# A decoder trunk in fp32: the additions behind seven products spread over more side steps, and the input loads put at the head of the queue

## The chip, the cores and the metric

The kernel runs on one core of one Trainium2 chip. The metric is the device time of one execution in microseconds; the median of three runs stands for a kernel. A profile is one further execution, recorded by the hardware profiler.

## What is computed

A two-layer trunk over 512 positions of width 2048, in fp32. Each layer is a half feed-forward block, a pair of mixers (attention in both layers, with a pooling mixer in the second), and another half feed-forward block, each behind an RMS norm and added to the residual. A last RMS norm gives the output. The part that matters here is the feed-forward block, with an inner width of 1536:

```python
def swiglu(x, w_gate, w_up, w_down):
    return (jax.nn.silu(x @ w_gate) * (x @ w_up)) @ w_down

h = h + 0.5 * swiglu(rms_norm(h, norm_g[i, 0]), ffn_w_gate[i, 0], ffn_w_up[i, 0], ffn_w_down[i, 0])
```

There are four such blocks. The first one is computed in the plain way (`ffn`), the other three by `ffn_products`.

## The kernel before

**Precision.** TensorE multiplies fp32r here. Every fp32 operand is therefore split into a high part (ScalarE, a copy, L273 for weights) and the rest (VectorE, a subtraction, L274), and a product is three matmuls: high by high, high by rest, rest by high (`mm3`, L302 to L304).

**Weights.** All weights come in a fixed sequence of tiles of at most 128x512 (`plan_and_uses`). A tile is loaded by SyncE's DMA queue into one of 9 buffers `raw` (L258) and split into one of 7 pairs `wh`, `wl`. `take` splits a tile six places ahead of the one that it hands to TensorE (`ahead`), so the split of tile i+6 stands on ScalarE and VectorE just ahead of the work that follows tile i. The load of a tile stands on SyncE's queue behind the release of the buffer nine tiles earlier.

**Three blocks with seven products.** The inner width is done in three units of 512 columns. For a unit, `w_gate` and `w_up` over the two halves of the 2048 rows, and the input over its two halves of positions, make a 2x2 by 2x2 block product, which is done with seven products instead of eight. Some weight tiles are first added to or subtracted from each other (L278). A unit has two passes. In the first (PSUM tiles `pa`), 24 weight tiles go through three products; in the second (`pb`), 32 tiles go through four. Each tile serves six matmuls of 128x128 by 512 columns. At the end of a pass the products are copied or added to SBUF tiles `s` (L612, L618).

**The additions.** What is left of a unit is `to_hidden` (L620 on), a generator: eight additions on VectorE (L622) and four Silu on ScalarE (L626, L629), then four multiplications on VectorE (L636) that give four tiles of rows, then, for each of four groups of 128 columns, four transposes of these rows on TensorE (L644, PSUM tile `ht`) and a split of the result into `hidh`, `hidl` (L312, L313). It is put into the deque `side` when the unit ends, and runs beside the next unit: each `tick()` advances it to its next `yield`. In the first pass of the next unit there is a tick behind each of the 24 weight tiles. Behind the third unit comes the down projection instead: its first four output tiles do the two units that are ready in eight half steps of 12 matmuls (`pd`), with two ticks behind each, then the deque is emptied (`while side: tick()`), and then the rest of these four tiles is done from the third unit.

The order of instructions on each engine is the order in which this code issues them; an engine works through its own in that order and waits where an operand isn't there.

**Start.** `load_x` (L349 to L352) loads the 16 tiles of the input, 128x512 each, on SyncE's queue, among the weight tiles. The first block needs x0 to x3 for its first four weight tiles, x4 to x7 for the next four, and so on. `beside(i)`, called behind weight tile i of the first block, splits input tile i+4 (`xgh` on ScalarE L315, `xgl` on VectorE L316) and adds the square of tile i to the norm's sum (ScalarE L387, GpSimd L395).

Of the kernel before, what the change touches and what calls it, by code (L numbers as in the profile page):

```python
# [216 lines left out]
def trunk(ctx: ExitStack, tc: tile.TileContext, xT, pos_row, pos_col, wts, gains, consts, bias_a_in, bias_b_in, outT):  # L217
# [19 lines left out]
    def blk(s, dt=F32):  # L237
        return bpool.tile([P, S], dt, tag="b", name=nm(s))

    def bank(s):  # L240
        return psum.tile([P, S], F32, tag="p", name=nm(s))
# [11 lines left out]
    def load_to(i):  # L253
        while nxt_load[0] <= min(i, len(plan) - 1):
            j = nxt_load[0]
            off, n = offsets[j]
            t = raws.tile([P, 512], F32, tag="raw", name=f"raw_{j}")
            nc.sync.dma_start(t[:, :n], wts[off:off + P * n].rearrange("(p n) -> p n", p=P))  # L258
            raw_t[j] = t
            nxt_load[0] += 1  # L260
# [25 lines left out]
    def take(name, n):  # L286

        while n:
            i = nxt_use[0]
            r = plan[i]  # L290
            assert r[0] == name and r[4] - r[3] <= n, (i, r, name, n)
            ahead()
            h, low = split_t.pop(i)
            w = offsets[i][1] // (r[4] - r[3])
            for k in range(r[4] - r[3]):
                c = slice(k * w, (k + 1) * w)
                yield r[3] + k, h[:, c], low[:, c]
            n -= r[4] - r[3]
            nxt_use[0] += 1

    def mm3(out, ah, al, bh, bl, start, stop):
        nc.tensor.matmul(out, ah, bh, start=start, stop=False)  # L302
        nc.tensor.matmul(out, ah, bl, start=False, stop=False)  # L303
        nc.tensor.matmul(out, al, bh, start=False, stop=stop)  # L304
# [34 lines left out]
    def finish(g):  # L339
        for _ in g:  # L340
            pass
# [7 lines left out]
    def load_x(d0, d1):  # L349
        for d in range(d0, d1):  # L350
            xs[d] = blk(f"x{d}")
            nc.sync.dma_start(xs[d], xT[d * P:(d + 1) * P, :])  # L352

    nc.scalar.dma_start(gn, gains)
    load_x(0, 4)
    load_to(2)
    load_x(4, 8)
    nc.scalar.dma_start(cs, consts)
    ident = cs[:, 0:P]
    mask_d = cs[:, P:2 * P]  # L360
# [16 lines left out]
    class Norm:  # L377
# [7 lines left out]
        def add(self, x, last=False):  # L385
            sq = blk("sq")[:, :self.m]
            nc.scalar.activation(sq, x, AF.Square)  # L387
            acc = self.accs[self.count % self.sums] if len(self.accs) >= self.sums else None
            self.count += 1
            if last or acc is None:  # L390
                self.accs.append(sq)
            elif self.by_dma:
                nc.gpsimd.dma_start(acc, sq, accum_op=ALU.add)
            else:
                nc.gpsimd.tensor_tensor(acc, acc, sq, op=ALU.add)  # L395
# [135 lines left out]
    def down_half(pd, job, hid, n):  # L531
        _, c0, c1 = job
        for k, wh, wl in take("ffn_w_down", n):
            mm3(pd[:, :c1 - c0], wh, wl, hid[k][0][:, c0:c1], hid[k][1][:, c0:c1], k == 0, k == NF - 1)
# [60 lines left out]
    def ffn_products(pieces, norm, resid_in, sink, down):  # L595
        hid = {}
        ng = norm.stages()
        both = range(2)
        late = pieces.late()

        def product(names, piece, ps, k, u):
            for kk, wh, wl in take(names, 1):
                assert kk % HK == k
                sh, sl = pieces.get(k, piece, u == FF // UNIT - 1)
                for a in both:
                    c = slice(a * P, a * P + P)
                    mm3(ps[a], sh[:, c], sl[:, c], wh, wl, k == 0, k == HK - 1)

        def copied(ps):
            out = [blk("s") for _ in both]  # L610
            for a in both:
                nc.scalar.activation(out[a], ps[a], AF.Copy)  # L612
            return out

        def added(ps, s, into=None):
            out = [blk("s") if into is None else into[a] for a in both]
            for a in both:
                nc.vector.tensor_tensor(out[a], ps[a], s[a], op=ALU.add)  # L618
            return out

        def to_hidden(u, c11, u2, s4, s5, s7, c12):
            add = lambda o, a, b: nc.vector.tensor_tensor(o, a, b, op=ALU.add)  # L622
            for a in both:
                add(s7[a], s7[a], u2[a])
                add(s4[a], s4[a], s7[a])
                nc.scalar.activation(s4[a], s4[a], AF.Silu, scale=norm.r[:, a:a + 1])  # L626
                yield
                add(s7[a], s7[a], s5[a])
                nc.scalar.activation(s7[a], s7[a], AF.Silu, scale=norm.r[:, 2 + a:3 + a])  # L629
                add(c12[a], c12[a], s5[a])  # L630
                yield
            u2.clear()
            s5.clear()
            for a in both:
                for o, g, r in ((c11, s4, a), (c12, s7, 2 + a)):
                    nc.vector.scalar_tensor_tensor(o[a], o[a], norm.r[:, r:r + 1], g[a], op0=ALU.mult, op1=ALU.mult)  # L636
                yield
            s4.clear()
            s7.clear()
            rows = c11 + c12  # L640
            for f in range(UNIT // P):
                pt = bank("ht")
                for b in range(NST):
                    nc.tensor.transpose(pt[:, b * P:b * P + P], rows[b][:, f * P:f * P + P], ident)  # L644
                yield
                hid[u * (UNIT // P) + f] = split(pt, "hid")

        for u in range(FF // UNIT):
            p1, p2, p4 = ([bank("pa") for _ in both] for _ in range(3))
            last = HK - 1  # L650
            for k in range(HK):
                product("ffn_w_up", "B11", p1, k, u)
                if k == last:
                    s1 = copied(p1)
                if u == 0:
                    for e in range(k + 1, min(k + 4, HK)):
                        pieces.get(e, "B11", False)
                else:
                    tick()
                product("ffn_w_up", "B21", p2, k, u)  # L660
                if k == last:
                    c11 = added(p2, s1)
                if u == 0:
                    next(late, None)
                else:
                    tick()
                product("ffn_w_gate", "T4", p4, k, u)
                if k == last:
                    s4 = copied(p4)
                if u:  # L670
                    tick()
                elif k > HK // 2:
                    next(ng, None)
            if u == 0:
                finish(ng)
                finish(late)
            del p1, p2, p4
            p5, p7, p6, p3 = ([bank("pb") for _ in both] for _ in range(4))
            for k in range(HK):
                product("ffn_w_gate", "T1", p5, k, u)  # L680
                if k == last:
                    s5 = copied(p5)
                if k % 2:
                    tick()
                product("ffn_w_gate", "T3", p7, k, u)
                if k == last:
                    s7 = copied(p7)
                if k % 2:
                    tick()
                product("ffn_w_up", "T2", p6, k, u)  # L690
                if k == last:
                    u2 = added(p6, s1, s1)
                if k % 2:
                    tick()
                product("ffn_w_up", "B22", p3, k, u)
                if k % 2:
                    tick()
            side.append(to_hidden(u, c11, u2, s4, s5, s7, added(p3, u2)))
            del p5, p7, p6, p3, s1, c11, u2, s4, s5, s7
        pds = [bank("pd") for _ in range(FIRST)]  # L700
        for pd, job in zip(pds, down):
            for n in (4, 4):
                down_half(pd, job, hid, n)
                tick(2)
        while side:
            tick()
        for pd, job in zip(pds, down):
            down_half(pd, job, hid, 4)
            down_done(pd, job, resid_in, sink)
        for job in down[FIRST:]:  # L710
            pd = bank("pd")
            for n in (8, 4):
                down_half(pd, job, hid, n)
                tick()
            down_done(pd, job, resid_in, sink)
# [222 lines left out]
        xg[d] = split(xs[d], "xg", scale=g_norm(0)(d))  # L938

    def beside(i):  # L940
        if i in (0, 3):
            load_x(8 if i == 0 else 12, 12 if i == 0 else 16)
        if i + 4 < NK:
            split_x(i + 4)
        norm.add(xs[i])
# [277 lines left out]
```

## Time and profile before

| | |
|---|---|
| median of 3 runs | 2327.6 us (2327.45 to 2329.95) |
| the profiled execution, its own time | 2328.22 us |
| its span, first to last instruction | 2326.4 us |
| TensorE matmuls (PE), busy | 2249.4 us, 97% |
| VectorE (DVE), busy | 1450.0 us, 62% |
| ScalarE (ACT), busy | 1051.5 us, 45% |
| mean granted TensorE clock | 0.984 |

In a row of the waits stand: engine, what it was about to write and its line, what it waited for; microseconds in total, times, longest. In a row of a timeline: start in us, busy us, engine, line, operation, output<-inputs, shape, count of merged instructions, and in brackets the idle time just before and what ended it. `SPq` is SyncE's DMA queue. In a row of the windows: from:to and length in us, then busy us and number of instructions of each engine, the granted clock (PEclk, 1.00 is full), the DMA share and GB/s.

### The profile page before, as it was taken

The page shows a single profiled execution, that of the slowest core. Times are in us where ns is not written, and L with a number is a line of the kernel's source. Part 1 is how long each engine was busy: PE and PEld are TensorE (multiplying, and loading weights), DVE is VectorE, ACT ScalarE, POOL GpSimd, SP SyncE. Part 2 cuts the span into 40 slices and gives each one's busy share as a digit, 9 for nine tenths or more (in the row PEclk, how much of TensorE's full clock was granted, in tenths as well). Part 3 has the DMA queues.
Part 4 walks back from the last instruction along what each step waited for, and adds up shares of the span by engine and source line. Part 5 has one row for each costly group of instructions (what it writes and reads, how often), then busy time and mean ns, then how long its engine had stood idle before and what let it go on. Part 6 is the DMA issues. An engine that isn't in the chain of part 4 may idle for free.

```text
span 2326.4 us, 30133 instructions
## 1 busy us (share of the span) xinstructions
PE 2249.4 (97%) x10364; PEld 1882.2 (81%) x10364; DVE 1450.0 (62%) x2460; ACT 1051.5 (45%) x1875; POOL 185.7 (8%) x191
## 2 busy tenths in 40 slices
PE   8999999999999999889999898999999999898997
PEld 6888888989888888778788787788888888687787
DVE  5453344464645688878557787755345679788634
ACT  5332333333334575445446454433235576454443
POOL 3000011000001011000011000011200011000013
PEclk9999999999999999999999999999999999999999
DMA  6333343423224486556676565554332486565544
GB/s 219 100 87 105 104 127 114 122 64 104 74 73 124 134 250 185 166 153 185 179 192 182 165 189 152 156 181 151 98 96 69 127 238 200 154 181 164 148 140 142
DMA packets 193290, 336.94 MB, mean 145 GB/s; under 512 B 21488, under 2 KB 44400, under 8 KB 193136
## 3 DMA queue, kind: packets, MB, share of 16 engines
q1 hardware_dynamic: 163184, 280.89, 40.9%
q10 hardware_dynamic: 23904, 43.11, 5.7%
q0 software_dynamic: 6048, 11.01, 2.9%
q8 instruction: 81, 1.33, 0.2%
q14 instruction: 73, 0.60, 0.1%
HBM read 298.75 MB, written 25.17 MB: 139 GB/s over the span
## 4 chain that ended last, share of the span: by engine, by line
PE 87%; DVE 5%; issue 3%; ACT 2%; DMA 2%; POOL 0%; DVEq 0%; ACTq 0%; POOLq 0%
PE pd L303 7%; PE pd L304 7%; PE pd L302 7%; PE pb L302 5%; PE pb L304 5%; PE pb L303 5%; PE pj L302 4%; PE pj L304 4%; PE pj L303 4%; PE pa L302 3%; PE pa L303 3%; PE pa L304 3%; PE wo L302 3%; PE wo L304 3%; PE wo L303 3%
## 5 line engine op out<-in xcount | busy, mean ns | idle before, releaser
L274 DVE TENSOR_TENSOR wl<-raw,wh 128x512 fp32r<-128x512 f32 (+3 forms) x1087 | 737.2, 688 | 605.1 <-ACT wh L273 569.2
L273 ACT ACTIVATE wh<-raw 128x512 fp32r<-128x512 f32 (+3 forms) x1087 | 652.5, 609 | 749.5 <-DVE wl L274 126.3
L302 PE MATMUL pd<-hidh,wh 128*128 128x512 f32 (+1 forms) x816 | 307.9, 377 | 0.0
L304 PE MATMUL pd<-hidh,wl 128*128 128x512 f32 (+1 forms) x816 | 307.3, 377 | 0.0
L303 PE MATMUL pd<-hidl,wh 128*128 128x512 f32 (+1 forms) x816 | 307.3, 377 | 0.0
L278 DVE TENSOR_TENSOR raw<-raw,raw 128x512 f32<-128x512 f32 x288 | 196.6, 683 | 0.0
L302 PE MATMUL pj<-xgh,wh 128*128 128x512 f32 x464 | 181.7, 392 | 0.0
L304 PE MATMUL pj<-xgh,wl 128*128 128x512 f32 x464 | 180.8, 390 | 0.0
L303 PE MATMUL pj<-xgl,wh 128*128 128x512 f32 x464 | 180.7, 389 | 0.0
L302 PEld LDWEIGHTS pd<-hidh,wh 128*128 128x128 f32 x816 | 153.6, 188 | 28.1
L303 PEld LDWEIGHTS pd<-hidl,wh 128*128 128x128 f32 x816 | 153.6, 188 | 28.0
L304 PEld LDWEIGHTS pd<-hidh,wl 128*128 128x128 f32 x816 | 153.6, 188 | 27.8
L302 PE MATMUL pa<-wh,pbh 128*128 128x512 f32 x432 | 175.1, 405 | 0.0
L395 POOL TENSOR_TENSOR sq<-sq,sq 128x512 f32<-128x512 f32 (+1 forms) x65 | 81.5, 1253 | 1155.8 <-ACT sq L387 1155.8
L303 PE MATMUL pa<-wl,pbh 128*128 128x512 f32 x432 | 171.6, 397 | 0.0
L304 PE MATMUL pa<-wh,pbl 128*128 128x512 f32 x432 | 171.3, 397 | 0.0
L302 PE MATMUL pb<-wh,pth 128*128 128x512 f32 x288 | 112.2, 390 | 0.9 <-DVE s L618 0.9
L304 PE MATMUL pb<-wh,ptl 128*128 128x512 f32 x288 | 112.0, 389 | 0.0
L303 PE MATMUL pb<-wl,pth 128*128 128x512 f32 x288 | 112.0, 389 | 0.0
L304 PEld LDWEIGHTS pj<-xgh,wl 128*128 128x128 f32 x464 | 87.1, 188 | 18.2
L303 PEld LDWEIGHTS pj<-xgl,wh 128*128 128x128 f32 x464 | 87.2, 188 | 17.4
L302 PEld LDWEIGHTS pj<-xgh,wh 128*128 128x128 f32 x464 | 87.2, 188 | 17.3
(265 smaller groups left out, 3941.6 us busy)
## 6 DMA issues: line engine op xcount, KB each, us to landing
raw<-wts SPq DMA_DIRECT2D x940, 256.0 KB, 2.8
spill<-x ACTq DMA_DIRECT2D x80, 256.0 KB, 3.0
x<-spill ACTq DMA_DIRECT2D x80, 256.0 KB, 3.1
raw<-wts SPq DMA_DIRECT2D x83, 192.0 KB, 2.4
sq<-sq POOLq DMA_DIRECT2D x42, 256.0 KB, 4.9
raw<-wts SPq DMA_DIRECT2D x48, 128.0 KB, 2.4
x<-xT SPq DMA_DIRECT2D x16, 256.0 KB, 5.0
outT<-sc SPq DMA_DIRECT2D x16, 256.0 KB, 2.3
```

Source lines behind the costliest of these rows:

```text
L273: nc.scalar.activation(h, src, AF.Copy)
L274: nc.vector.tensor_tensor(low, src, f32(h), op=ALU.subtract)
L278: nc.vector.tensor_tensor(to, a, b, op=ALU.add if sign > 0 else ALU.subtract)
L302: nc.tensor.matmul(out, ah, bh, start=start, stop=False)
L303: nc.tensor.matmul(out, ah, bl, start=False, stop=False)
L304: nc.tensor.matmul(out, al, bh, start=False, stop=stop)
L395: nc.gpsimd.tensor_tensor(acc, acc, sq, op=ALU.add)
```

## The change

Two things. In `to_hidden` more `yield` statements are put in: where a step of additions or multiplications was followed by one, there are now two, and one more stands ahead of the transposes. The generator has 17 of them where it had 10. And the 16 input tiles are all loaded at the start, four at a time with two weight tiles behind each four; `beside` loads none any more.

```diff
     nc.scalar.dma_start(gn, gains)
-    load_x(0, 4)
-    load_to(2)
-    load_x(4, 8)
+    for i in range(4):
+        load_x(4 * i, 4 * i + 4)
+        load_to(2 * i + 2)
...
                 nc.scalar.activation(s4[a], s4[a], AF.Silu, scale=norm.r[:, a:a + 1])
                 yield
+                yield
                 add(s7[a], s7[a], s5[a])
                 nc.scalar.activation(s7[a], s7[a], AF.Silu, scale=norm.r[:, 2 + a:3 + a])
                 add(c12[a], c12[a], s5[a])
+                yield
                 yield
...
                     nc.vector.scalar_tensor_tensor(o[a], o[a], norm.r[:, r:r + 1], g[a], op0=ALU.mult, op1=ALU.mult)
                 yield
+                yield
             s4.clear()
             s7.clear()
+            yield
...
     def beside(i):
-        if i in (0, 3):
-            load_x(8 if i == 0 else 12, 12 if i == 0 else 16)
         if i + 4 < NK:
             split_x(i + 4)
```

**TensorE, the first pass of the second unit** (the first of six such places). Before, these rows stand behind 7 of the pass's 24 weight tiles, that is behind 42 matmuls; `wh_8382` is the seventh tile, and `s` are the four tiles of rows:

```order
L304 MATMUL pa_8377<-wh_8382,pbl_7233 128x512
L644 MATMUL ht_8482<-cs,s_7919 128x128
L644 MATMUL ht_8482<-cs,s_7920 128x128
L644 MATMUL ht_8482<-cs,s_8372 128x128
L644 MATMUL ht_8482<-cs,s_8373 128x128
L302 MATMUL pa_8378<-wh_8397,pbh_7236 128x512
```

Now they stand behind 14 tiles, that is behind 84 matmuls; `wh_8478` is the fourteenth tile:

```order
L304 MATMUL pa_8379<-wh_8478,pbl_7405 128x512
L648 MATMUL ht_8566<-cs,s_7919 128x128
L648 MATMUL ht_8566<-cs,s_7920 128x128
L648 MATMUL ht_8566<-cs,s_8372 128x128
L648 MATMUL ht_8566<-cs,s_8373 128x128
L302 MATMUL pa_8380<-wh_8490,pbh_7400 128x512
```

The same four transposes moved by seven weight tiles; the three groups behind them still follow one per tile. Beside the down projection the first group moved from behind four half steps to behind seven, and the last three groups now stand in one piece behind the eighth, just ahead of the matmuls that use them.

**VectorE, the same place.** Before, one split of a weight tile (L274) stands between two steps of the additions:

```order
L274 TENSOR_TENSOR wl_8383<-raw_8258,wh_8382 128x512
L622 TENSOR_TENSOR s_8342<-s_8342,s_7902 128x512
L622 TENSOR_TENSOR s_7943<-s_7943,s_8342 128x512
L274 TENSOR_TENSOR wl_8398<-raw_8270,wh_8397 128x512
L622 TENSOR_TENSOR s_8342<-s_8342,s_8326 128x512
L622 TENSOR_TENSOR s_8372<-s_8372,s_8326 128x512
L274 TENSOR_TENSOR wl_8413<-raw_8282,wh_8412 128x512
L622 TENSOR_TENSOR s_8343<-s_8343,s_7903 128x512
```

Now there are two:

```order
L274 TENSOR_TENSOR wl_8383<-raw_8258,wh_8382 128x512
L622 TENSOR_TENSOR s_8342<-s_8342,s_7902 128x512
L622 TENSOR_TENSOR s_7943<-s_7943,s_8342 128x512
L274 TENSOR_TENSOR wl_8398<-raw_8270,wh_8397 128x512
L274 TENSOR_TENSOR wl_8410<-raw_8282,wh_8409 128x512
L622 TENSOR_TENSOR s_8342<-s_8342,s_8326 128x512
L622 TENSOR_TENSOR s_8372<-s_8372,s_8326 128x512
L274 TENSOR_TENSOR wl_8425<-raw_8294,wh_8424 128x512
L274 TENSOR_TENSOR wl_8437<-raw_8306,wh_8436 128x512
L622 TENSOR_TENSOR s_8343<-s_8343,s_7903 128x512
```

From the first addition to the last multiplication five more splits stand in between. ScalarE's high parts follow the same pattern between its Silu. Beside the down projection, where two ticks followed each split, one step now stands between two splits.

**SyncE's queue, the start.** Before, behind the input tiles x4 to x7 (the last of them is `x_8`), these weight tiles follow, the fourth to the ninth:

```order
L352 DMA x_8_100<-xT 128x512
L258 DMA raw_112<-wts 128x512
L258 DMA raw_114<-wts 128x512
L258 DMA raw_116<-wts 128x512
L258 DMA raw_118<-wts 128x512
L258 DMA raw_120<-wts 128x512
L258 DMA raw_122<-wts 128x512
```

Now two weight tiles follow, then the input tiles x8 to x11, two weight tiles, and the next input tiles:

```order
L352 DMA x_8_100<-xT 128x512
L258 DMA raw_102<-wts 128x512
L258 DMA raw_104<-wts 128x512
L352 DMA x_9_106<-xT 128x512
L352 DMA x_10_108<-xT 128x512
L352 DMA x_11_110<-xT 128x512
L352 DMA x_12_112<-xT 128x512
L258 DMA raw_114<-wts 128x512
L258 DMA raw_116<-wts 128x512
L352 DMA x_13_118<-xT 128x512
```

Before, x8 to x11 stood behind 16 weight tiles and x12 to x15 behind 19. The sixth and seventh weight tile now have four more input tiles ahead of them, the eighth and ninth eight more.

## The prediction

> **What bounds the kernel now.** First the page, for the engine that sets the time:
>
> ```profile
> span 2326.4 us, 30133 instructions
> PE 2249.4 (97%) x10364; PEld 1882.2 (81%) x10364; DVE 1450.0 (62%) x2460; ACT 1051.5 (45%) x1875; POOL 185.7 (8%) x191
> ```
>
> TensorE works through 97% of the span, so what can be won here lies in its gaps. The waits of TensorE name them:
>
> ```profile
> PE ht L644 <- DVE s L636: 53.4, 21, 7.3
> PE gu L303 <- DVE xgl L316: 2.4, 1, 2.4
> ```
>
> The transposes wait 53.4 us for VectorE's rows, nearly all that TensorE waits for. The order shows nine such places: six passes and three starts of a down projection. The windows give the length of each from its first matmul on. First the six units with two passes, of which three and the sum are shown:
>
> ```profile
> 920.25:1009.77 89.52, 80.78 (x354) 66.05 (x352) 70.45 (x112) 44.91 (x73) 0.00 (x0) 0.94 0.60 165
> 1009.77:1098.23 88.46, 81.05 (x354) 66.27 (x352) 70.46 (x112) 43.63 (x72) 0.00 (x0) 0.94 0.59 166
> 1994.55:2084.51 89.96, 81.22 (x354) 66.38 (x352) 70.45 (x112) 45.08 (x73) 0.00 (x0) 0.94 0.57 164
> sum 532.83, PE 485.67 PEld 397.04 DVE 422.63 ACT 264.97 POOL 0.00; mean PE 80.95 PEld 66.17 DVE 70.44 ACT 44.16 POOL 0.00
> ```
>
> Then the three starts of a down projection, up to the ninth half step, one and the sum:
>
> ```profile
> 1098.23:1124.51 26.28, 24.18 (x114) 19.62 (x112) 18.02 (x29) 9.57 (x16) 0.00 (x0) 1.00 0.35 94
> sum 78.76, PE 72.48 PEld 58.81 DVE 54.05 ACT 28.72 POOL 0.00; mean PE 24.16 PEld 19.60 DVE 18.02 ACT 9.57 POOL 0.00
> ```
>
> The granted clock of 0.94 in the passes says that each also runs at half clock for a while. TensorE's timeline in the second of these units shows why:
>
> ```profile
> 1009.77 0.39 PE L302 MATMUL pa<-wh,pbh 128*128 128x512 f32 x1
> ...
> 1019.06 0.39 PE L304 MATMUL pa<-wh,pbl 128*128 128x512 f32 x1
> 1025.40 0.47 PE L644 MATMUL ht<-cs,s 128*128 128x128 f32 x1 [5.96 <-DVE s L636]
> 1027.33 1.14 PE L644 MATMUL ht<-cs,s 128*128 128x128 f32 x3 [1.45 <-DVE s L636]
> 1028.12 0.78 PE L302 MATMUL pa<-wh,pbh 128*128 128x512 f32 x1
> 1028.70 0.63 PE L303 MATMUL pa<-wl,pbh 128*128 128x512 f32 x1
> 1029.12 0.63 PE L304 MATMUL pa<-wh,pbl 128*128 128x512 f32 x1
> ...
> 1033.37 0.60 PE L644 MATMUL ht<-cs,s 128*128 128x128 f32 x4
> ...
> 1035.20 0.60 PE L644 MATMUL ht<-cs,s 128*128 128x128 f32 x4
> ```
>
> From 1009.77 to 1019.06 start 42 matmuls, 41 steps of 0.227 us, so a weight tile (six) takes 1.36. Behind seven tiles the transposes come and stand for about 8 us. Then matmuls start 0.42 to 0.43 apart, half the pace. An undisturbed group of transposes is read at the end: 1.83 us from group to group, less 1.36, is 0.47.
>
> So a unit without loss would be 56 tiles x 1.36 + 4 x 0.47 = 78.05 us, six of them 468.3; lost are 532.8 - 468.3 = 64.5 us, of it the waits and the slow clock behind them. A down start would be 8 x 12 x 0.227 + 4 x 0.47 = 23.7, three 71.0; lost are about 7.8 us. Together 72.3 us can be won, and no more.
>
> **The additions: where they end.** VectorE and ScalarE in the same pass, their timelines:
>
> ```profile
> 1012.14 0.68 DVE L274 TENSOR_TENSOR wl<-raw,wh 128x512 fp32r<-128x512 f32 x1
> 1012.74 1.41 DVE L622 TENSOR_TENSOR s<-s,s 128x512 f32<-128x512 f32 x2
> 1015.46 0.69 DVE L274 TENSOR_TENSOR wl<-raw,wh 128x512 fp32r<-128x512 f32 x1 [1.31 <-DMA raw<-wts]
> 1016.07 1.28 DVE L622 TENSOR_TENSOR s<-s,s 128x512 f32<-128x512 f32 x2
> ...
> 1026.53 1.41 DVE L636 SCALAR_TENSOR_TENSOR s<-s,r,s 128x512 f32<-128x512 f32 x2
> 1027.86 1.28 DVE L274 TENSOR_TENSOR wl<-raw,wh 128x512 fp32r<-128x512 f32 x2
> ```
>
> ```profile
> 1014.18 0.72 ACT L626 ACTIVATE s<-s,r 128x512 f32<-128x512 f32 x1 [3.58 <-DVE s L622]
> 1014.81 0.61 ACT L273 ACTIVATE wh<-raw 128x512 fp32r<-128x512 f32 x1
> ...
> 1023.35 2.17 ACT L273 ACTIVATE wh<-raw 128x512 fp32r<-128x512 f32 x4
> ```
>
> This is a chain that hands over between the two engines: additions at 1012.74, Silu at 1014.18, the next high part queued behind it at 1014.81, its rest at 1015.46 (the wait is put down to a load, but the high part had just started), the next additions at 1016.07. It doesn't wait for TensorE, and ends at 1027.94, 18.17 us after the pass began. The change puts one more split into each of the five gaps. Its high part follows the other 0.52 later ((2.17 - 0.61) / 3) and is hidden; its rest takes VectorE's pace, 0.60 (1012.14 to 1012.74). So the chain grows by 5 x 0.60 = 3.0 and ends at 21.17.
>
> TensorE now reaches the transposes behind 14 tiles, at 14 x 1.36 = 19.04. Before, it resumed 0.18 behind the chain's end (1028.12); so it resumes at 21.35 instead of 19.04 + 0.47 = 19.51, a loss of 1.84 us. Where the wait goes, the weights could be late next. The rest of tile 11 (counted from 0) starts behind the third step: that step was at 1018.67 - 1009.77 = 8.90, becomes 10.10, then two additions and Silu (1.44), 0.63 and 0.65 make 12.82, ready at 13.5; TensorE wants it at 14.96. Tile 13 is ready at 16.7, wanted at 17.68. The cover is 1 us.
>
> ```profile
> 1018.67 1.41 DVE L622 TENSOR_TENSOR s<-s,s 128x512 f32<-128x512 f32 x2
> ```
>
> Two of the six have one instruction more on ScalarE (x73):
>
> ```profile
> 924.70 1.28 ACT L626 ACT_TABLE_LOAD   x1 [3.62 <-DVE s L622]
> ```
>
> With its handover it puts the chain back by 1.33 (Silu at 926.00 - 920.25 = 5.75, against 1014.18 - 1009.77 = 4.41). There the loss is 3.17, and tile 13 comes some 0.2 late, inside the same wait, since the chain and not TensorE sets its end.
>
> **The clock.** Does TensorE fall to half clock behind these shorter waits? Windows of 3.41 us on the grid on which the clock changes, with a gap at the start and the one at a down projection:
>
> ```profile
> 21.97:25.38 3.41, 1.00 (x5) 0.52 (x4) 3.41 (x4) 0.79 (x2) 2.05 (x2) 1.00 0.72 268
> 25.38:28.79 3.41, 3.41 (x10) 2.62 (x9) 2.08 (x4) 1.76 (x3) 1.27 (x1) 0.50 0.95 315
> 1107.40:1110.81 3.41, 2.17 (x10) 1.35 (x8) 2.70 (x5) 1.79 (x4) 0.00 (x0) 1.00 0.11 19
> 1110.81:1114.23 3.42, 2.57 (x14) 2.08 (x15) 2.97 (x5) 1.61 (x3) 0.00 (x0) 1.00 0.33 83
> ```
>
> A window with 1.00 us of work was followed by half clock, windows with 2.17 and 2.57 were not. A loss of 1.84 leaves about 1.6 of work in a window at worst and usually straddles two: full clock, by the nearer row. A loss of 3.17 can leave 0.3 to 1.6: one window of half clock, 1.7 us, each. The Trainium skill ("TensorE: Matmul & The Clock Gate", the part on the HAM clock gate) has the clock fall after at least one idle window of about 3.4 us. By that rule neither would fall and the sum would be 3.4 us lower; the window with 1.00 us of work speaks against it.
>
> So the six units keep 4 x 1.84 + 2 x (3.17 + 1.7) = 17.1 of their 64.5.
>
> **The down starts.** Here one split per step stands between the steps, as in the old passes, so the chain again ends near 18.2, and TensorE arrives behind seven half steps, 7 x 12 x 0.227 = 19.04. No wait; the cover is 0.9 us. The other twelve transposes now run in one piece ahead of the matmuls that read them; the last group's split, high part and rest of 0.6 to 0.7 each, has the matmuls of three earlier groups (0.68 each) beside it. I take 0.3 us for each start, between 0 and 1.3 (both parts uncovered): 0.9 kept of 7.8.
>
> **The start.** This half of the change costs. ScalarE's timeline, then VectorE's, then TensorE's:
>
> ```profile
> 12.34 2.67 ACT L273 ACTIVATE wh<-raw 128x512 fp32r<-128x512 f32 x4 [2.76 <-DMA raw<-wts]
> ...
> 16.05 0.62 ACT L273 ACTIVATE wh<-raw 128x512 fp32r<-128x512 f32 x1
> 16.57 0.71 ACT L315 ACTIVATE xgh<-x,gn 128x512 fp32r<-128x512 f32 x1
> ```
>
> ```profile
> 23.10 1.75 DVE L316 SCALAR_TENSOR_TENSOR xgl<-x,gn,xgh 128x512 fp32r<-128x512 f32 x1
> ```
>
> ```profile
> 22.09 0.40 PE L302 MATMUL gu<-xgh,wh 128*128 128x512 f32 x1
> 24.90 0.50 PE L303 MATMUL gu<-xgl,wh 128*128 128x512 f32 x1 [2.41 <-DVE xgl L316]
> ```
>
> The fourth to seventh weight tile (the first row) were split as they landed, one per (2.67 - 0.63) / 3 = 0.68 us. The eighth now has eight input tiles more ahead of it: it was 4 behind the fourth, is 12, and lands at 12.34 + 12 x 0.68 = 20.5 where its split was at 16.05. The splits of x5 to x7 stand behind it on ScalarE, so everything up to the last `xgl` moves by 4.4 us, and with it the matmul at 24.90. Nothing gains from the earlier x8 to x15: TensorE waits for none of them. I take 4.4; if VectorE's slow splits there (1.75 for what is 0.75 elsewhere) come faster when spread out, it is near 1; one or two windows more of half clock make it 6 to 8.
>
> **The sum.** 72.3 - 17.1 - 0.9 - 4.4 = 49.9 us gained. The profiled execution took 2328.2, its span and 1.8 around it, so 2278.3; it stands 0.6 over the median, which makes 2277.7 us.
>
> **The rivals.**
> - *Full clock throughout.* No window of half clock behind the two longer waits: 3.4 less, 2274.3. For it: at 3.17 us each is shorter than a window of 3.41. Against it: the window with 1.00 us of work. Chance 0.15. This is the case that the rule of the Trainium skill (same title and part) makes.
> - *Half clock everywhere.* The waits of 1.84 fall into one window each and trip the clock, the long ones for two windows: 4 x 1.7 + 2 x 1.7 = 10.2 more, 2287.9. For it: 46% of work in a window lies between the rows above, and neither decides. Chance 0.15.
> - *The rows come in time.* If the extra splits find gaps in the chain (VectorE is idle 1.3 us ahead of the split at 1015.46) and cost nothing, it ends at 18.17, before 19.04, and only the start's 4.4 and the 0.9 are kept: 2327.6 - 67.0 = 2260.6. Against it: each gap waits for the Silu behind the additions, and a split put ahead of the additions delays both. Chance 0.08.
> - *Slower: the splits hold the chain.* The place is ScalarE's high part: seven pairs `wh`, `wl` are all there are, and if each added split has to wait until TensorE has done two more tiles, a step grows by 2.72 instead of 0.60. The chain then ends at 18.17 + 5 x 2.72 = 31.8, TensorE waits 12.7 and loses 2.2 at half clock; six times 14.9 is 89.4, against 64.5 now. With the start's 4.4 and 6.9 won at the down starts: 2327.6 + 24.9 + 4.4 - 6.9 = 2350. It decides from 2.1 us per step on. Against it: in this stretch every ScalarE row waits for VectorE and none for TensorE, and tile 13 needs the pair of tile 6, done at 9.5, where its split now comes at 15.4. Chance 0.04.
>
> **How the numbers follow.** The forecast has 0.56. All cases but the last lie 39 us or more below the kernel before; 0.02 are left for a mishap of just its size. What a measurement of this kernel can tell from no change is about 0.2%, 4.7 us: faster 0.94, same 0.02, slower 0.04. The range holds the forecast with its bounds, the start (-3.4, +3.6) and the steps of the chain (0.2 us in each of five, 1 us at each of six places, 6 in all), and both clock cases: 2277.7 - 3.4 - 3.4 - 6 = 2265 to 2277.7 + 3.6 + 10.2 + 6 = 2297. Left out are the third and fourth rival.
>
> **What would show it.** In the profile after: transposes waiting for the multiplications for some 2 us in four passes and 3 us in two, instead of 8; no wait of that kind at the down starts; units of about 80 us; the matmul that stood until 24.90 now near 29.3, behind the same `xgl`. It is wrong if TensorE waits for `wl` or `wh` in a first pass (the cover of 1 us was none), if the chain ends elsewhere than 21 us into a pass, or if the clock falls behind waits of under 2 us.

## The result, and the profile after

The changed kernel takes 2277.25 us (median of 4 runs, 2276.64 to 2278.01) where the kernel before took 2327.57 in the same runs: a ratio of 0.9782 with a 95% interval of 0.9765 to 0.9799. The profiled execution took 2276.7 us, with a span of 2274.8.

The page, as far as it answers to the lines of before:

```profile
span 2274.8 us, 30119 instructions
PE 2237.3 (98%) x10364; PEld 1874.3 (82%) x10364; DVE 1442.1 (63%) x2460; ACT 1047.0 (46%) x1875; POOL 185.4 (8%) x191
```

TensorE's waits, the three longest:

```profile
PE ht L648 <- DVE s L638: 10.9, 12, 2.2
PE gu L302 <- ACT xgh L315: 7.3, 2, 5.8
PE gu L303 <- DVE xgl L316: 4.0, 3, 2.0
```

The wait of the transposes went from 53.4 to 10.9 us. The two waits of the first block (`gu`) grew; before, they were 5.9 and 2.4. The windows of the units, each from the first matmul of a unit to that of the next, again three of the six and the sum:

```profile
925.76:1007.05 81.29, 78.82 (x353) 64.49 (x352) 69.10 (x112) 44.22 (x73) 0.00 (x0) 1.00 0.63 182
1007.05:1087.02 79.97, 78.48 (x354) 64.56 (x352) 69.12 (x112) 43.05 (x72) 0.00 (x0) 1.00 0.63 185
1961.74:2044.50 82.76, 80.28 (x354) 65.55 (x352) 69.59 (x112) 44.25 (x73) 0.00 (x0) 0.98 0.61 178
sum 483.96, PE 473.00 PEld 388.30 DVE 415.11 ACT 260.68 POOL 0.00; mean PE 78.83 PEld 64.72 DVE 69.18 ACT 43.45 POOL 0.00
```

And the sum over the three starts of a down projection:

```profile
sum 70.42, PE 70.42 PEld 58.76 DVE 47.88 ACT 25.74 POOL 0.00; mean PE 23.47 PEld 19.59 DVE 15.96 ACT 8.58 POOL 0.00
```

The units are 48.9 us shorter (532.8 to 484.0), the down starts 8.3 us (78.8 to 70.4; TensorE is busy through all of it), and the first unit begins 5.5 us later (920.25 to 925.76). Together these make 51.7 us; between the two spans lie 51.6.

TensorE in the second of these six units, at the moved transposes:

```profile
1026.10 0.27 PE L648 MATMUL ht<-cs,s 128*128 128x128 f32 x1
1027.63 0.44 PE L648 MATMUL ht<-cs,s 128*128 128x128 f32 x2 [1.26 <-DVE s L638]
1028.29 0.33 PE L648 MATMUL ht<-cs,s 128*128 128x128 f32 x1 [0.23 <-DVE s L638]
1028.38 0.48 PE L302 MATMUL pa<-wh,pbh 128*128 128x512 f32 x1
```

VectorE in the same pass, the last step but one and the last:

```profile
1024.30 1.41 DVE L638 SCALAR_TENSOR_TENSOR s<-s,r,s 128x512 f32<-128x512 f32 x2
1025.63 1.28 DVE L274 TENSOR_TENSOR wl<-raw,wh 128x512 fp32r<-128x512 f32 x2
1026.83 1.41 DVE L638 SCALAR_TENSOR_TENSOR s<-s,r,s 128x512 f32<-128x512 f32 x2
```

Two splits now stand between two multiplications. The last of these ends at 1028.24, which is 21.19 us into the pass; TensorE goes on at 1028.38, 21.33 into it. The first transpose of the group needs a row that is there; the second waits 1.26 us for a row of the last step.

At the start, TensorE and ScalarE:

```profile
20.00 0.39 PE L304 MATMUL gu<-xgh,wl 128*128 128x512 f32 x1
21.85 0.49 PE L302 MATMUL gu<-xgh,wh 128*128 128x512 f32 x1 [1.46 <-ACT xgh L315]
...
26.00 0.80 PE L303 MATMUL gu<-xgl,wh 128*128 128x512 f32 x1 [2.00 <-DVE xgl L316]
...
29.35 0.80 PE L303 MATMUL gu<-xgl,wh 128*128 128x512 f32 x1 [1.71 <-DVE xgl L316]
```

```profile
16.42 1.32 ACT L273 ACTIVATE wh<-raw 128x512 fp32r<-128x512 f32 x2 [2.75 <-DMA raw<-wts]
17.64 0.71 ACT L315 ACTIVATE xgh<-x,gn 128x512 fp32r<-128x512 f32 x1
...
20.55 0.63 ACT L273 ACTIVATE wh<-raw 128x512 fp32r<-128x512 f32 x1 [1.68 <-DMA raw<-wts]
21.09 0.70 ACT L315 ACTIVATE xgh<-x,gn 128x512 fp32r<-128x512 f32 x1
```

ScalarE waits for the sixth weight tile until 16.42 and for the eighth until 20.55, and the input tile x5 can be split only behind the latter. The matmul that stood until 24.90 now stands until 29.35.

### The profile page after: what moved, and what is told of

It reads as the page before. It is cut to its first block, busy times and chain, and to the rows that moved or that the text cites. A ratio compares the mean times of both kernels' runs of the same rounds, so it can differ in the third digit from the quotient of the medians.

```text
span 2274.8 us, 30119 instructions
## 1 busy us (share of the span) xinstructions
PE 2237.3 (98%) x10364; PEld 1874.3 (82%) x10364; DVE 1442.1 (63%) x2460; ACT 1047.0 (46%) x1875; POOL 185.4 (8%) x191
## 4 chain that ended last, share of the span: by engine, by line
PE 93%; DVE 3%; issue 1%; ACT 1%; DMA 0%; POOL 0%; DVEq 0%; ACTq 0%; POOLq 0%
PE pd L303 8%; PE pd L302 8%; PE pd L304 8%; PE pb L302 6%; PE pb L303 6%; PE pb L304 6%; PE pj L302 5%; PE pj L304 5%; PE pj L303 5%; PE pa L302 4%; PE pa L304 3%; PE pa L303 3%; PE wo L302 3%; PE wo L304 3%; PE wo L303 3%; PE pr L302 2%
## 5 line engine op out<-in xcount | busy, mean ns | idle before, releaser
L274 DVE TENSOR_TENSOR wl<-raw,wh 128x512 fp32r<-128x512 f32 (+3 forms) x1087 | 733.2, 687 | 564.7 <-ACT wh L273 529.8
L278 DVE TENSOR_TENSOR raw<-raw,raw 128x512 f32<-128x512 f32 x288 | 196.6, 682 | 0.0
```

Of the source, the lines that this page charges most:

```text
L274: nc.vector.tensor_tensor(low, src, f32(h), op=ALU.subtract)
L278: nc.vector.tensor_tensor(to, a, b, op=ALU.add if sign > 0 else ALU.subtract)
```

## The experiments

The theory: the steps of the additions, the Silu and the weight splits queued between them form one chain over VectorE and ScalarE that TensorE doesn't pace; TensorE waits only where it comes to the transposes before that chain's end. The loads at the start are a cost apart. The rivals: the two parts are tied together; the pace of the additions is worth nothing, only the place of the transposes; or whatever is moved, the wait moves along with it.

**Only the loads at the start.** Against the kernel before.

```diff
-    load_x(0, 4)
-    load_to(2)
-    load_x(4, 8)
+    for i in range(4):
+        load_x(4 * i, 4 * i + 4)
+        load_to(2 * i + 2)
...
-        if i in (0, 3):
-            load_x(8 if i == 0 else 12, 12 if i == 0 else 16)
```

> Only the loads at the start are changed, the additions stay as they were. Theory (the eighth weight tile now lands behind eight more input tiles, and the splits of x5 to x7 queue behind it): slower than the kernel before by the 5.5 us by which the first unit's start moved between the two profiles (920.25 to 925.76), 2333.1 us; TensorE's last wait for xgl ends near 29.3 and not at 24.9. Rival (the loads are hidden and the 5.5 us come from elsewhere): 2327.6 us.

Measured: 2333.61 us against 2328.81 for the kernel before, ratio 1.0020 (1.0012 to 1.0029). Slower, by 4.8 us; the first of the six units starts at 925.15 us of the profile, where it was 920.25. The last wait for `xgl` ends at 29.25, and the transposes wait 53.4 us as in the kernel before. The loads cost by themselves.

**Only the additions spread.** The changed kernel with the loads of before.

```diff
-    for i in range(4):
-        load_x(4 * i, 4 * i + 4)
-        load_to(2 * i + 2)
+    load_x(0, 4)
+    load_to(2)
+    load_x(4, 8)
...
+        if i in (0, 3):
+            load_x(8 if i == 0 else 12, 12 if i == 0 else 16)
```

> Only the additions are spread, the loads at the start are those of before. Theory (the two parts add up): 2277.3 - 5.5 = 2271.8 us; first unit from 920.2 us on, transposes waiting for the rows as in the changed kernel, some 11 us in all. Rival (the parts are tied together, the earlier input tiles help later): 2277 us.

Measured: 2273.11 us, ratio 0.9759 (0.9746 to 0.9773); the transposes wait 10.9 us in all, the first unit starts at 920.34. The two parts multiply to 1.0020 x 0.9759 = 0.9779, where the whole change has 0.9782. As far as these intervals tell, the parts are independent, and the first takes back 4.8 of the 55.7 us that the second gives.

**The old pace, only the transposes late.** Is the spreading itself worth anything? Against the kernel before.

```diff
             s4.clear()
             s7.clear()
+            for _ in range(7):
+                yield
             rows = c11 + c12
```

> The additions keep the old pace, one split of a weight tile between two steps; only the transposes move, by seven ticks, to the same place behind 14 weight tiles. Start as before. Theory (the steps hold back the weight splits queued behind them on ScalarE): the rows are there at 18.2 us into a pass, before TensorE arrives, so no wait for rows; but the rest of the weight tiles 10 to 13 comes 0.6 to 1.1 us late, TensorE waits for wl instead and loses about 2.3 us in four passes and 3.6 in two, a little more than with the spread additions: 2274 us. Rival (the place of the transposes is all that counts, the pace is worth nothing): no wait left, 2271.8 - 14 = 2258 us.

Measured: 2274.65 us, ratio 0.9770 (0.9756 to 0.9783), not to be told from the spread additions by its time. The rival's 2258 is out. TensorE's waits:

```profile
PE pa L303 <- DVE wl L274: 5.0, 20, 0.3
PE pa L302 <- ACT wh L273: 3.9, 8, 0.6
PE gu L303 <- DVE xgl L316: 3.3, 2, 2.4
PE ht L646 <- DVE hidl L313: 1.9, 3, 1.3
```

No wait for rows is left; in its place TensorE waits 28 times for weight tiles. One of these, the first in the second of the six units:

```profile
1017.12 0.39 PE L304 MATMUL pa<-wh,pbl 128*128 128x512 f32 x1
1017.96 0.50 PE L302 MATMUL pa<-wh,pbh 128*128 128x512 f32 x1 [0.46 <-ACT wh L273]
1018.69 0.50 PE L303 MATMUL pa<-wl,pbh 128*128 128x512 f32 x1 [0.22 <-DVE wl L274]
```

VectorE in the same pass, two of its weight splits and the last multiplications:

```profile
1009.40 0.69 DVE L274 TENSOR_TENSOR wl<-raw,wh 128x512 fp32r<-128x512 f32 x1 [1.31 <-ACT wh L273]
...
1012.01 0.69 DVE L274 TENSOR_TENSOR wl<-raw,wh 128x512 fp32r<-128x512 f32 x1 [0.71 <-ACT wh L273]
...
1020.48 1.41 DVE L636 SCALAR_TENSOR_TENSOR s<-s,r,s 128x512 f32<-128x512 f32 x2
```

The chain ends at 1021.89, 18.17 us after this pass began at 1003.72, exactly as in the kernel before, and the transposes come after that. But at this pace one weight tile is split per step of the chain, here 2.6 us apart, while TensorE uses one per 1.36; with the spread additions it is two per step. So the transposes' place takes away the wait for rows, and the slower pace keeps the weights in time. By the windows the six units lose 20.6 us, against 17.4 with the spread additions; this profiled execution lay 3.1 us over its median, so the difference is not clear of noise. The gain of the change is that of the later place; the spreading alone buys nothing here that the times show. There is also a wait that was not expected, for `hidl`; the next run shows it at its clearest.

**Spread, and the transposes three ticks later still.** Against the changed kernel; the loads are those of before.

```diff
...
             s4.clear()
             s7.clear()
-            yield
+            for _ in range(4 if u < FF // UNIT - 1 else 1):
+                yield
             rows = c11 + c12
...
```

> The additions spread as in the changed kernel, and in the first passes (not beside the down projection) the transposes three ticks later, behind 17 weight tiles. Start as before. Theory (the chain of additions ends at 21.2 us into a pass, 22.5 with the table load, by the splits between its steps and not by TensorE): TensorE arrives at 23.1, no wait for rows is left but some 0.2 to 0.4 us for a weight tile in two passes; against the spread alone 4 x 1.9 + 2 x 3.2 and 1.7 of half clock less: 2256 us, no half clock in any pass. Rival (the chain gives way as TensorE does, the wait moves along with the transposes or on to the weights): 2268 to 2272 us.

Measured: 2268.24 us, ratio 0.9739 (0.9725 to 0.9752), at the rival's 2268 and 12 us over the theory's. TensorE's first wait, and one place in its timeline:

```profile
PE ht L649 <- DVE hidl L313: 7.7, 6, 1.9
```

```profile
1029.09 0.40 PE L304 MATMUL pa<-wh,pbl 128*128 128x512 f32 x1
1030.40 0.66 PE L649 MATMUL ht<-cs,s 128*128 128x128 f32 x4 [0.91 <-DVE hidl L313]
```

The wait for rows is gone, as the theory has it, and none for weights has come. Still the six units lose 13.9 us, and two of them have a window of half clock, which was not expected either. The third of the four groups of transposes now waits for the split of the first. The first pass holds six of the eight banks in the kernel's PSUM pool, so the groups alternate between two, and a bank comes free when `hidl` has read it. VectorE at that time:

```profile
1023.64 3.09 DVE L274 TENSOR_TENSOR wl<-raw,wh 128x512 fp32r<-128x512 f32 x5
1026.65 0.68 DVE L278 TENSOR_TENSOR raw<-raw,raw 128x512 f32<-128x512 f32 x1
...
1028.46 0.68 DVE L274 TENSOR_TENSOR wl<-raw,wh 128x512 fp32r<-128x512 f32 x1
1029.07 0.68 DVE L278 TENSOR_TENSOR raw<-raw,raw 128x512 f32<-128x512 f32 x1
1029.67 0.68 DVE L313 TENSOR_TENSOR hidl<-ht,hidh 128x512 fp32r<-128x512 f32 x1
```

It is working off the splits that stood behind the additions, and the last tiles of the pass bring a sum (L278) each. `hidl` stands behind them, comes at 1029.67 and ends at 1030.35, and the transposes start at 1030.40. The theory was right on the chain and lacked this step.

**The loads of x8 to x15 behind the weights.** What is it in the loads that costs? Against the kernel before.

```diff
     load_x(0, 4)
     load_to(2)
     load_x(4, 8)
+    load_to(8)
+    load_x(8, 16)
...
-        if i in (0, 3):
-            load_x(8 if i == 0 else 12, 12 if i == 0 else 16)
```

> The kernel before, with one change: the input tiles x8 to x15 are loaded at the start as in the changed kernel, but behind the first nine weight tiles and not among them. Theory (the cost at the start comes from weight tiles six to nine, which land behind eight input tiles): they land as before, TensorE's last wait for xgl ends near 24.9, and the time is that of the kernel before, within 1 us. Rival (loading all input at once is what costs, by a busy queue): slower by about 5 us, as with the loads among the weight tiles.

Measured: 2326.92 us against 2328.71, ratio 0.9989 (0.9980 to 0.9997); the first unit starts at 919.57. ScalarE splits the fourth to seventh weight tile from 12.61 on without a gap, and the eighth at 16.31. Loading the input early costs nothing when the weights stand ahead of it; the cost was that of the four weight tiles that had come to stand behind input tiles. The run was even 1.8 us faster, where no difference beyond 1 us was expected, and the last wait for `xgl` ended at 24.25, not near 24.9; why stays open.

**The groups of transposes apart.** If two banks and a late `hidl` are what is left, groups two tiles apart should be free of both. Against the changed kernel; the loads are those of before.

```diff
...
             s4.clear()
             s7.clear()
-            yield
+            for _ in range(3 if u < FF // UNIT - 1 else 1):
+                yield
             rows = c11 + c12
...
                 hid[u * (UNIT // P) + f] = split(pt, "hid")
+                if u < FF // UNIT - 1:
+                    yield
...
```

> Start as before, additions spread as in the changed kernel; in the first passes the transposes come behind 16 weight tiles, and the four groups stand two weight tiles apart instead of one. Theory (with the transposes three ticks later, the third group waited for its PSUM bank, which the rest hidl of the first group frees, and that stands on VectorE behind weight splits and their sums; two tiles apart this has time): no wait for hidl, and for rows only some 0.9 us in the two passes with the table load; the six units lose about 3 us instead of 17.4 with the spread alone, 2273.1 - 14 = 2259 us. Rival (VectorE as a whole is the bound of the pass, whatever is moved makes it late elsewhere): the units lose 12 us or more, 2266 to 2268 us.

Measured: 2257.01 us, ratio 0.9690 (0.9677 to 0.9703), faster than the kernel before and than the spread additions alone (0.9759). No wait of the transposes is left in TensorE's list. The first two units:

```profile
921.21:999.88 78.67, 78.61 (x354) 64.51 (x353) 67.84 (x112) 44.01 (x73) 0.00 (x0) 1.00 0.63 188
999.88:1077.96 78.08, 78.08 (x354) 64.65 (x353) 68.26 (x112) 42.78 (x72) 0.00 (x0) 1.00 0.65 189
```

TensorE is busy throughout the second one. By the windows the six units lose 1.3 us in all, against 64.5 in the kernel before and 15.7 in the changed one. VectorE has 68 of 78 us of work there, so it is not the bound that the rival made of it: it was the order of the instructions that made TensorE wait. Whether the old pace would do as well with its transposes spaced like this was not run.

## Why the prediction was right, step by step

**The chain.** Predicted to end 21.17 us into a pass, by 0.60 for each of five more splits; measured 21.19. TensorE was to go on at 21.35 and did at 21.33. The loss of a unit was to be 1.84 and 3.17 us; the windows less the 78.05 give 1.92 and 3.24. That it is the splits that lengthen the chain was shown by the run with the old pace: without them its chain ended at 18.17.

**The cover of the weights.** It held: no wait for `wl` or `wh` stands in the changed kernel's list, though the cover was 1 us. The run with the old pace shows what lies beyond it.

**The clock.** One window of half clock was charged for each of the two longer waits. It came in one of them (82.76 against 81.29, 1.5 us) and not in the other; without the changed loads, where the grid of windows falls otherwise, it came in both. The units kept 15.7 us and not 17.1. The waits of 1.84 tripped nothing, as forecast, but with less room than the prediction thought. They left 1.92 to 2.11 us of work in a window; a window with the 1.6 that it named as the worst would, by the 1.72 at the start (last section), probably have tripped the clock. The second unit:

```profile
1024.92:1028.33 3.41, 1.92 (x10) 1.13 (x10) 3.41 (x7) 1.90 (x4) 0.00 (x0) 1.00 0.70 236
```

**The down starts.** No wait, as predicted: the chain ended 18.18 us into the first of them and TensorE came to the transposes at 19.05. But the 0.3 us kept per start was a charge too many: the sum of 70.4 lies 0.6 under the 71.0 that were taken as free of loss, since twelve transposes in one piece take 1.23 us, from 1109.26 to 1110.49, and not 3 x 0.47.

```profile
1109.26 1.47 PE L648 MATMUL ht<-cs,s 128*128 128x128 f32 x12
1110.49 0.47 PE L302 MATMUL pd<-hidh,wh 128*128 128x512 f32 x1
```

**The start.** The eighth weight tile was to land at 20.5 and its split came at 20.55; the last wait moved by 4.45 us, as the 4.4 had it. The cost was 5.5, since TensorE also had half clock from 24.81 to 35.05, three windows where it had been one. The prediction put one or two windows more at 6 to 8 us in all and left that out of the sum. Its term was too small by 1.1 us, and its bound too large: up to 29.35 the half clock cost nothing, since `xgl` set the end of that wait. Behind it half clock lasted 5.70 us, from 29.35 to 35.05, where it had lasted 3.41; half of the difference is about the missing 1.1. The run with the loads alone agrees:

```profile
23.53:33.77 10.24, 6.72 (x15) 4.44 (x16) 8.30 (x8) 5.40 (x10) 5.31 (x5) 0.50 0.53 182
```

There 4.52 us at half clock lie behind the last wait, which had moved by 4.35; with 0.55, half of 4.52 - 3.41, this gives the 4.9 us by which its first unit came later. That the cost comes from the place of four weight tiles was shown by the two runs on the loads.

**The sum.** These errors, 1.4 and 1.5 us one way and 1.1 the other, leave 1.8 us, and most of that is undone because this profiled execution lay 0.6 under its median where that of before lay 0.6 over. The terms were right in kind and each within 1.5 us; that the forecast lies half a microsecond from the median is luck.

## What to carry to other kernels

Where an engine that works in order stands at an instruction whose inputs come from a chain on other engines, write down when that chain ends, and put the instruction just behind that time; what was queued inside the chain counts towards it, step by step. Then look at what the moved instruction holds or needs next: here first the weights behind the Silu, then two PSUM banks that a late read kept. Loads for later must not stand ahead of loads that the next split waits for.

## What the hardware showed that was not expected

The clock fell behind windows in which TensorE had worked for a part, not only behind idle ones. The granted clock changes on a grid of windows of 3.41 us (24.81 to 35.05 is three of them), and windows that were partly busy were followed by half clock or not. In the changed kernel, at the start and in the first and the fifth unit:

```profile
21.40:24.81 3.41, 1.72 (x4) 0.67 (x4) 3.12 (x4) 3.41 (x7) 2.01 (x2) 1.00 1.05 385
24.81:35.05 10.24, 7.35 (x16) 5.31 (x17) 7.12 (x7) 4.23 (x8) 4.52 (x4) 0.50 0.47 135
946.41:949.82 3.41, 1.92 (x9) 1.46 (x10) 3.41 (x6) 0.93 (x2) 0.00 (x0) 1.00 0.56 169
1980.65:1984.06 3.41, 1.21 (x6) 0.53 (x4) 3.41 (x6) 2.08 (x4) 0.00 (x0) 1.00 0.68 191
1984.06:1987.47 3.41, 3.18 (x10) 2.46 (x10) 3.21 (x6) 0.67 (x2) 0.00 (x0) 0.50 0.77 252
```

With the transposes three ticks later:

```profile
947.40:950.81 3.41, 1.51 (x9) 1.06 (x8) 3.41 (x7) 1.52 (x3) 0.00 (x0) 1.00 0.94 334
950.81:954.22 3.41, 3.41 (x11) 2.73 (x10) 3.41 (x6) 1.34 (x3) 0.00 (x0) 0.50 0.48 162
```

And with the old pace, near the end of the kernel, where the matmuls are shorter (128x256 and 128x1):

```profile
2259.60:2263.01 3.41, 2.15 (x19) 1.98 (x17) 1.18 (x3) 0.81 (x2) 0.13 (x1) 1.00 0.50 174
2263.01:2266.42 3.41, 0.69 (x2) 0.29 (x2) 1.28 (x2) 0.38 (x1) 3.05 (x3) 0.50 0.36 124
```

In the first two groups, windows with 1.21, 1.51 and 1.72 us of work were followed by half clock, one with 1.92 was not; there a bound would lie between 50% and 56% of a window. The last group shows that it is no general one: 2.15 us, 63%, were followed by half clock. The ends of matmuls are modelled, and a matmul that stands alone counts as 0.49 us (21.85) where in a row they start 0.227 apart, so the profile's busy time is not quite the work; what the clock goes by stays open. A wait of about 2.2 us trips it or not by where it falls on the grid: the first and the fifth unit have the same wait (2.19 and 2.20), and only the fifth lost 1.5 us more. The rule of the Trainium skill ("TensorE: Matmul & The Clock Gate", the part on the HAM clock gate), which asks for an idle window of about 3.4 us, is too lenient by these rows.
